# Three mixer gates computed as seven half-sized products by tokens

## The chip, the cores and the metric

The kernel runs on one core of one Trainium2 chip. The metric is device time in microseconds: 1072.74 us before, the median of 3 runs (1071.83 to 1073.14). Times inside the kernel come from one profiled execution.

## The reference

One decoder layer on 512 tokens of width 1024, in fp32. What matters here is the mixer's middle:

```python
proj = x @ w_in            # q/k/v columns of three branches, then 3 x 1024 gate columns
...
g = jax.nn.sigmoid(gates).reshape(B, S, N_BRANCHES, D)
merged = (g[:, :, 0] * (o_da @ w_branch_da) + g[:, :, 1] * (o_sb @ w_branch_sb)
          + g[:, :, 2] * (o_dl @ w_branch_dil))
return merged @ w_out
```

`o_da`, `o_sb` and `o_dl` (512 x 512 each) are the outputs of differential, stick-breaking and dilated attention. A layer norm of alpha * x + mixer(x) follows, then a squared-ReLU MLP (4096 wide), an embedding term with a gate of its own (sigmoid(x W_g), 1024 x 1024), and a second layer norm.

## The kernel before

**Arithmetic.** Each fp32 operand is split in a high half (cast to fp32r) and a low half (what the cast lost), and a product is three matmuls into one PSUM bank: high x high, high x low, low x high. For weights `split_next` does this: a cast on ScalarE (line 235) and a subtraction on VectorE (line 238) turn a raw tile of 128 x 1024 into `wh` and `wl`. Such a tile of 512 KB is called a chunk.

**Items.** The program is a list of items, made first and then walked in one loop (lines 1472 to 1525). An item is a run of matmuls into one bank (`mm`) and an evacuation (`ev`), which is issued when the next item begins. The items are, in order: 59 projections of q, k and v (main_order), of 24 matmuls each; the mixer gates (24 items `gate` of 24 matmuls each, columns in partitions, tokens along the free axis) with the branch products (24 items of 12 matmuls, `branch_items`) between them, two blocks of 128 columns ahead; the output projection (`wout_items`, 8 items of 24); the embedding's gate and the embedding (`wg_items`, `ple_items`); the MLP. Walking the list, `step` advances the attention heads, which are generators; a yield inside `mm` is one more step.

**Loads.** `fill` issues loads of raw tiles on SyncE's queue (SP) as far as raw tiles are free: 4 of them (RAW). `pump` splits up to 7 chunks (RING) ahead of the last freed one. A load waits in SP's queue until a split has freed its tile, and what is issued behind it on SP waits too.

**Seven products.** The embedding's gate and the MLP already use a scheme by which a product of 2 x 2 blocks takes seven half-sized products instead of eight. It needs sums of weight blocks. `totals` lists them, and `add` issues one at a time while the items go by: a copy of a block to a DRAM tile on SP's queue, then sums into it by an accumulating DMA on GpSimd's queue (POOL, line 176). `add` is called once per 3 units of item size from item 24 on. The sums of the activation blocks are made in SBUF, in `ln1_gen`, from transposes of the normed tokens.

**Merging.** For each of 8 column blocks the evacuation of a branch product applies the sigmoid to the gate (`gate_sig`, tied behind the last exponential of the differential attention), multiplies and adds; after the third branch the block is split in halves (`mh`, `ml`), and these stand still in the output projection without a transpose.

**Places.** 48 SBUF tiles of 128 x 512 are shared under the tag "s"; two large tiles (tags XH and XL) hold the halves of x transposed, and later those of the normed tokens; two PSUM banks `mm` and six `at`.

Of the kernel before, what the change touches and what calls it, by code (L numbers as in the profile page):

```python
# [17 lines left out]
P = 128  # L18
# [16 lines left out]
def main_order():  # L35
# [14 lines left out]
    for j in range(8):  # L50
        for i in range(3):
            o += [("T", "gate", 8 * i + j)]
# [3 lines left out]
def trunk(tc, a, out):  # L56
    nc = tc.nc
    es = ExitStack()
    with es:
# [7 lines left out]
        NSLOT = 48  # L67
# [74 lines left out]
        RING, RAW = 7, 4  # L142
        ORDERED, AHEAD = 17, 4
        loads, sums, chunks, placed = [], deque(), [], []
# [7 lines left out]
        def totals(quads):  # L152
# [5 lines left out]
            for o, i, more in ((0, 0, False), (2, 1, False), (0, 1, True), (2, 3, True), (1, 3, False), (3, 2, False)):  # L158
                for (q, x) in zip(quads, t):
                    sums.append((x[o], q[i], more))  # L160
            for o in (1, 3):
                for x in t:
                    sums.append((x[o], x[0 if o == 1 else 1][:, :], True))
            return [{1: q[0], 2: q[2], 3: q[3], 4: x[3], 5: x[0], 6: x[1], 7: x[2]} for q, x in zip(quads, t)]
# [3 lines left out]
        def add():  # L168
            if not sums:
                return  # L170
            t, s, more = sums.popleft()
            if not more:
                wide = [x.rearrange("(a b) m -> a (b m)", b=4) for x in (t[:, :], s)]
                nc.sync.dma_start(*wide)
                return
            i = nc.gpsimd.dma_start(t, s, accum_op=OP.add, max_dma_last_dim=2048)  # L176
            tc.add_manual_dep(getattr(i, "ins", i), casts[0].name, mybir.DependencyInfo(
                mybir.DependencyClass.Sync, mybir.DependencyReason.DATA), reason="one sum at a time")

        def chunk_of(s):  # L180
            c = {"from": s, "w": s["w"]}
            s["uses"] += 1
            chunks.append(c)
            return c
# [4 lines left out]
        def fill():  # L189
            while st["dma"] < len(loads):  # L190
                s = loads[st["dma"]]
                while any(t is s["src"] for t, _, _ in sums):
                    add()
# [75 lines left out]
        gate_raw = {}  # L269
# [16 lines left out]
        def t_evac(name, j):  # L286
            def ev(ps):
# [5 lines left out]
                elif name == "gate":  # L293
                    t = slot("graw")
                    cp(t, ps)
                    gate_raw[j] = t
# [75 lines left out]
        for kind, name, j in order[2:]:  # L372
            if kind == "T":
                if name == "gate":
                    continue
# [10 lines left out]
        sg = {}  # L386

        last_exp = [None]

        def gate_sig(i, j):  # L390
            t = gate_raw.pop(8 * i + j)

            with tc.issue_after(last_exp[0]):
                nc.scalar.activation(t, t, AF.Sigmoid)
            sg[i, j] = t

        def branch_items(j, between=()):
            c1 = chunk(a["wb1"][j].rearrange("p k m -> p (k m)"), 1024)
            c2 = chunk(a["wb2"][j].rearrange("p k m -> p (k m)"), 512)
            for n, i in enumerate((1, 2, 0)):  # L400
                if n == 2:
                    for t in between:
                        t_item(*t)
                    if j == 0:
                        first_da.append(len(items))
                def mm(ps, i=i):
                    c = c2 if i == 2 else c1
                    for k in range(4):
                        s = slice(((i % 2) * 4 + k) * P, ((i % 2) * 4 + k) * P + P)
                        h, lo = oTs[4 * i + k]  # L410
                        mm3(ps, c["h"][:, s], c["l"][:, s], h, lo, k == 0, k == 3)

                def ev(ps, i=i, n=n):
                    gate_sig(i, j)
                    g = sg.pop((i, j))
                    nc.vector.tensor_mul(g, g, ps)
                    if n == 0:
                        merged[j] = g
                    else:
                        nc.vector.tensor_add(merged[j], merged[j], g)  # L420
                    if n == 2:
                        m = merged[j]
                        h = slot("mh", F32R)
                        lo = slot("ml", F32R)
                        nc.scalar.copy(h, m)
                        nc.vector.tensor_sub(lo, m, h.bitcast(F32))
                        merged[j] = (h, lo)
                item([c1, c2] if n == 2 else [], mm, ev, need=[c1, c2], size=2)

        first_branch = [None]  # L430
        first_da = []
        LEAD = 2
        gates = [(j, i) for j in range(8) for i in range(3)]
        for j in range(LEAD):
            for i in range(3):
                t_item(nt, "gate", 8 * i + j)
                nt += 1
        first_branch[0] = len(items)
        for j in range(8):

            gs = [(nt + i, "gate", 8 * i + j + LEAD) for i in range(3)] if j + LEAD < 8 else []
            nt += len(gs)
            branch_items(j, gs if j == 0 else ())
            if j:
                for t in gs:
# [1178 lines left out]
```

## Time and profile before

| What | Value |
|---|---|
| median of 3 runs | 1072.74 us (1071.83 to 1073.14) |
| the profiled execution, its own time and its span | 1073.58 us, 1071.8 us |
| TensorE busy, instructions | 1056.0 us (99%), 5543 |
| VectorE, ScalarE busy | 719.9 us (67%), 528.3 us (49%) |
| moved by DMA | 203.87 MB, 190 GB/s on average |

In the lines of the page, a row of a group gives line, engine and operation, out<-in by tile names, shapes, and the count after x; then busy time and mean length of one in ns, then the idle time of the engine ahead of them and what ended it. A row of busy time by stretch gives start:end, length, then each engine's busy time with its instructions, the granted TensorE clock, the DMA engines' busy share and GB/s. A row of single instructions gives start and length in us. Bars of matmuls overlap, so their length is not what one costs. The projections end near 445 us, gates and branches run to 646 us, the output projection to 691, the embedding with its gate to 744.

### The profile page before, as it was taken

The page shows a single profiled execution, that of the slowest core. Times are in us where ns is not written, and L with a number is a line of the kernel's source. Part 1 is how long each engine was busy: PE and PEld are TensorE (multiplying, and loading weights), DVE is VectorE, ACT ScalarE, POOL GpSimd, SP SyncE. Part 2 cuts the span into 40 slices and gives each one's busy share as a digit, 9 for nine tenths or more (in the row PEclk, how much of TensorE's full clock was granted, in tenths as well). Part 3 has the DMA queues.
Part 4 walks back from the last instruction along what each step waited for, and adds up shares of the span by engine and source line. Part 5 has one row for each costly group of instructions (what it writes and reads, how often), then busy time and mean ns, then how long its engine had stood idle before and what let it go on. Part 6 is the DMA issues. An engine that isn't in the chain of part 4 may idle for free. (4 is left out here: it accounts for less than half of the span.)

```text
span 1071.8 us, 14697 instructions
## 1 busy us (share of the span) xinstructions
PE 1056.0 (99%) x5543; PEld 907.8 (85%) x5543; DVE 719.9 (67%) x1264; ACT 528.3 (49%) x866; POOL 83.0 (8%) x106
## 2 busy tenths in 40 slices
PE   8999999999999999999999999999999999999996
PEld 6888788999888888888888888888989989989985
DVE  5988577656443756655444445898786787787786
ACT  5665445435232545545333333375666567557551
POOL 0000200010011101011101110100100010000000
PEclk9999999999999999999999999999999999999999
DMA  7643545393777647575798757349989895655722
GB/s 275 189 175 123 174 166 134 122 255 98 236 217 199 192 139 209 172 204 163 202 259 226 189 160 243 110 132 279 245 215 258 253 257 194 196 177 178 236 79 79
DMA packets 61624, 203.87 MB, mean 190 GB/s; under 512 B 7387, under 2 KB 8299, under 8 KB 60465
## 3 DMA queue, kind: packets, MB, share of 16 engines
q1 hardware_dynamic: 41536, 164.03, 43.9%
q0 software_dynamic: 19440, 37.98, 20.5%
q8 instruction: 43, 0.70, 0.3%
q10 hardware_dynamic: 576, 0.92, 0.2%
q14 instruction: 29, 0.23, 0.1%
HBM read 200.78 MB, written 73.42 MB: 256 GB/s over the span
## 5 line engine op out<-in xcount | busy, mean ns | idle before, releaser
L235 ACT CAST wh<-raw 128x1024 fp32r<-128x1024 f32 (+1 forms) x231 | 238.9, 1036 | 296.6 <-PE mm L88 159.5
L238 DVE TENSOR_TENSOR wl<-raw,wh 128x1024 fp32r<-128x1024 f32 (+1 forms) x231 | 277.2, 1205 | 141.0 <-ACT wh L235 137.1
L87 PE MATMUL mm<-xhT,wh 128*128 128x512 f32 x496 | 196.4, 396 | 0.0
L89 PE MATMUL mm<-xhT,wl 128*128 128x512 f32 x496 | 194.2, 392 | 0.0
L88 PE MATMUL mm<-xlT,wh 128*128 128x512 f32 x496 | 194.0, 391 | 0.0
L89 PEld LDWEIGHTS mm<-xhT,wl 128*128 128x128 f32 x496 | 93.2, 188 | 19.6
L87 PEld LDWEIGHTS mm<-xhT,wh 128*128 128x128 f32 x496 | 93.3, 188 | 19.3 <-issue 1.1
L88 PEld LDWEIGHTS mm<-xlT,wh 128*128 128x128 f32 x496 | 93.3, 188 | 17.9
L744 PE MATMUL mm<-x1hT,wh 128*128 128x256 f32 x256 | 72.5, 283 | 2.4 <-DVE cut L756 2.4
L746 PE MATMUL mm<-x1hT,wl 128*128 128x256 f32 x256 | 72.5, 283 | 0.0
L745 PE MATMUL mm<-x1lT,wh 128*128 128x256 f32 x256 | 72.5, 283 | 0.0
L348 PE MATMUL mm<-wh,xhT 128*128 128x512 f32 x160 | 64.8, 405 | 0.0
L350 PE MATMUL mm<-wh,xlT 128*128 128x512 f32 x160 | 63.2, 395 | 0.0
L349 PE MATMUL mm<-wl,xhT 128*128 128x512 f32 x160 | 63.0, 394 | 0.0
L744 PE MATMUL mm<-xs,wh 128*128 128x256 f32 x192 | 54.5, 284 | 0.0
L745 PE MATMUL mm<-xs,wh 128*128 128x256 f32 x192 | 54.4, 283 | 0.0
L746 PE MATMUL mm<-xs,wl 128*128 128x256 f32 x192 | 54.3, 283 | 0.0
L176 POOL DMA_DIRECT2D total<-total x34 | 30.2, 954 | 278.7 <-ACT wh L235 233.1
L744 PEld LDWEIGHTS mm<-x1hT,wh 128*128 128x128 f32 x256 | 49.1, 192 | 2.8 <-issue 2.6
L745 PEld LDWEIGHTS mm<-x1lT,wh 128*128 128x128 f32 x256 | 49.1, 192 | 0.3
L746 PEld LDWEIGHTS mm<-x1hT,wl 128*128 128x128 f32 x256 | 49.2, 192 | 0.0
L350 PEld LDWEIGHTS mm<-wh,xlT 128*128 128x128 f32 x160 | 37.9, 237 | 3.9
(388 smaller groups left out, 2187.1 us busy)
## 6 DMA issues: line engine op xcount, KB each, us to landing
raw<-total SPq DMA_DIRECT2D x68, 512.0 KB, 4.3
raw<-in_wt_dram SPq DMA_DIRECT2D x62, 512.0 KB, 4.8
total<-total POOLq DMA_DIRECT2D x34, 512.0 KB, 9.5
total<-in_wu_dram SPq DMA_DIRECT2D x32, 512.0 KB, 6.8
total<-in_wd_dram SPq DMA_DIRECT2D x28, 512.0 KB, 6.6
raw<-in_wd_dram SPq DMA_DIRECT2D x25, 512.0 KB, 4.5
raw<-in_wu_dram SPq DMA_DIRECT2D x24, 512.0 KB, 4.6
raw<-in_wv_dram SPq DMA_DIRECT2D x20, 512.0 KB, 4.5
```

Source lines behind the costliest of these rows:

```text
L87: nc.tensor.matmul(ps, wh, xh, start=start, stop=False, skip_group_check=True)
L88: nc.tensor.matmul(ps, wh, xl, start=False, stop=False, skip_group_check=True)
L89: nc.tensor.matmul(ps, wl, xh, start=False, stop=stop, skip_group_check=True)
L176: i = nc.gpsimd.dma_start(t, s, accum_op=OP.add, max_dma_last_dim=2048)
L235: i = nc.vector.tensor_copy(h, raw) if c.get("dve") else nc.scalar.copy(h, raw)
L238: i = nc.vector.tensor_sub(lo, raw, h.bitcast(F32))
L348: nc.tensor.matmul(ps, x1, c["h"][:, s], start=k == 0, stop=False)
L349: nc.tensor.matmul(ps, x1, c["l"][:, s], start=False, stop=False)
L350: nc.tensor.matmul(ps, x2, c["h"][:, s], start=False, stop=k == 7)
L744: nc.tensor.matmul(o, c["h"][:, s], h, start=first, stop=False, skip_group_check=True)
L745: nc.tensor.matmul(o, c["h"][:, s], lo, start=False, stop=False, skip_group_check=True)
L746: nc.tensor.matmul(o, c["l"][:, s], h, start=False, stop=last, skip_group_check=True)
```

## The change

- The three gates become 14 items each of 12 matmuls (`seven`): tokens stand still, weights move, and seven products (numbered 1 to 7) with two groups of 128 tokens each give the four blocks of a gate. A bank is held over products 1, 6, 7, 4 in an `at` bank (`chain`).
- x's block sums are made by `x_load` (quarters of x loaded again, 8 loads of 256 KB) and `x_sum` (sum, cast, lower half), hooked to the items at and after the first gate. Gate tiles stay in "s" until used.
- The first gate (stick-breaking) has its four weight sums made by DMA. For the other two (`mixed`) only two sums are made by DMA; products 6 and 4 add a raw tile to the one of product 5 in SBUF (`plus`, a tensor_add in `split_next`), with weights ordered 1, 5, 6, 3, 4, 7, 2 and used in the order 1, 5, 6, 3, 7, 4, 2.
- Order: gate, gate, dilated branch, gate, then the branches of differential and stick-breaking attention. The dilated branch runs ahead of the point where all attention has ended.
- Branch products are by tokens too: 8 items of 12 matmuls each. Attention outputs are kept whole and split shortly before use (`halves`). The sigmoid has no tie to the exponentials any more.
- Merged tokens are transposed (`turn`, 32 transposes) into tiles under the tags XH and XL, which the output projection reads; `fold4` puts the normed tokens' halves in the same place afterwards. The output projection has a yield in its middle.
- `add` keeps two lists: copies (on SP, each issued after the last load) up to 24 ahead of the sums, and alone before item 23; it starts at item 7, with rates by stretch (one per 2.3, 5, 3.2, 2.4 or 5.5 units of item size).
- 5 raw tiles instead of 4, 46 tiles "s" instead of 48. The one-hot rows are loaded on SP with the constants, at item 4, instead of on POOL's queue.

```diff
-        NSLOT = 48
+        NSLOT = 46
...
-        RING, RAW = 7, 4
+        RING, RAW = 7, 5
...
+            if mixed:
+                t = [(new(), new()) for _ in quads]
+                for o in range(2):
+                    for q, x in zip(quads, t):
+                        copies.append((x[o], q[3 * o]))
+                for o in range(2):
+                    for q, x in zip(quads, t):
+                        sums.append((x[o], q[1]))
+                return [{1: q[0], 2: q[2], 3: q[3], 5: x[0], 7: x[1]} for q, x in zip(quads, t)]
...
+        def add(only=False):
+            if copies and (only or moved[0] < moved[1] + LEAD):
+                moved[0] += 1
+                t, s = copies.popleft()
                 wide = [x.rearrange("(a b) m -> a (b m)", b=4) for x in (t[:, :], s)]
-                nc.sync.dma_start(*wide)
...
+                with tc.issue_after(st["load"]):
+                    nc.sync.dma_start(*wide)
+            elif sums and not only:
+                moved[1] += 1
+                t, s = sums.popleft()
+                i = nc.gpsimd.dma_start(t, s, accum_op=OP.add, max_dma_last_dim=2048)
...
+            if c["plus"]:
+                raw = c["from"]["raw"]
+                nc.vector.tensor_add(raw, raw, c["plus"]["raw"])
+                c["plus"]["uses"] -= 1
...
+        def seven(ws, ops, fin, two):
...
+                def mm(ps):
+                    q = slice(r * P, r * P + P)
+                    for k in range(4):
+                        c = cs[k // 2]
+                        s = slice((k % 2) * 512, (k % 2) * 512 + 512)
+                        h, lo = operand(ops, p, k, q)
+                        nc.tensor.matmul(ps, h, c["h"][:, s], start=k == 0 and begins, stop=False,
+                                         skip_group_check=True)
+                        nc.tensor.matmul(ps, h, c["l"][:, s], start=False, stop=False, skip_group_check=True)
+                        nc.tensor.matmul(ps, lo, c["h"][:, s], start=False, stop=k == 3 and ends,
+                                         skip_group_check=True)
...
+            def weights(p):
+                if 6 in ws:
+                    return [chunk(w, 1024) for w in ws[p]]
+                base, more = {6: (5, 3), 4: (5, 2)}.get(p, (p, None))
+                for q in (base, more):
+                    if q and q not in raw:
+                        raw[q] = [load(w, 1024) for w in ws[q]]
+                return [chunk_of(raw[base][c], more and raw[more][c]) for c in range(2)]
...
+                if 6 not in ws:
+                    made = {p: weights(p) for p in (1, 5, 6, 3, 4, 7, 2)}
+                    for p in (1, 5, 6, 3, 7, 4, 2):
+                        for r in range(2):
+                            one_item(p, r, made[p], {4: made[4] + made[7], 7: []}.get(p))
+                    return
...
+            nc.vector.tensor_tensor(src, i, j, op=o)
+            nc.scalar.copy(h, src)
+            nc.vector.tensor_sub(lo, src, h.bitcast(F32))
+
+        GATES = (1, 2, 0)
+        gate_w = [block_weights("wga", i, n > 0) for n, i in enumerate(GATES)]
...
+        gate(0)
+        gate(1)
+        branch(2, False)
+        gate(2)
+        first_branch = len(items)
+        branch(0, False)
+        branch(1, True)
...
+        def turn(tt):
+
+            yield
+            if not mT:
+                mT.extend(one.tile([P, 8, 512], F32R, name=nm(n), tag=n, bufs=1) for n in ("XH", "XL"))
+            q = slice(tt * P, tt * P + P)
+            for half in range(2):
+                tp = at_bank()
+                for b in range(4):
+                    nc.tensor.transpose(tp[:, b * P:b * P + P], merged[tt, half][:, b * P:b * P + P], ident)
+                t3 = tp.rearrange("p (k t) -> p k t", k=4)
+                h, lo = [b[:, 4 * half:4 * half + 4, q] for b in mT]
+                nc.scalar.copy(h, t3)
+                nc.vector.tensor_sub(lo, t3, h.bitcast(F32))
+            yield
...
-            if n >= 24 and not wout_at + 2 <= n < wout_at + 16:
+            if n >= 7 and not wout_at + 5 <= n < wout_at + 20:
                 due[0] += it["size"]
-                while due[0] >= 3:
-                    due[0] -= 3
-                    add()
+                rate = 2.3 if n < gates_at else 5 if n < gates_at + 14 else 3.2 if n < first_branch else 2.4 if n < wout_at else 5.5
+                while due[0] >= rate:
+                    due[0] -= rate
+                    add(n < 23)
```

More of the change, by code (lines that the diff above doesn't have):

```diff
@@ L385, in trunk @@
         merged = {}
[L386 to L407, printed above, removed]
+        at = {}
@@ L428, in branch_items @@
[L428 to L445, printed above, removed]
-                    t_item(*t)
+                        nc.tensor.matmul(ps, h[:, q], c["h"][:, s], start=k == 0, stop=False)
```

399 lines of the change are left out of this document (222 added, 177 removed).

## The prediction

> **What bounds the kernel now.** I read the head of the page first, then busy time by stretch, then single starts on TensorE.
>
> ```profile
> PE 1056.0 (99%) x5543; PEld 907.8 (85%) x5543; DVE 719.9 (67%) x1264; ACT 528.3 (49%) x866; POOL 83.0 (8%) x106
> ```
> ```profile
> core 0: us, PE busy (x) PEld busy (x) DVE busy (x) ACT busy (x) POOL busy (x), PEclk, DMA share, GB/s
> ...
> 25.00:445.00 420.00, 419.47 (x2068) 355.33 (x2067) 277.10 (x640) 201.56 (x390) 33.56 (x42) 1.00 0.59 175
> 445.00:510.00 65.00, 65.00 (x325) 54.37 (x324) 35.46 (x79) 32.45 (x71) 9.11 (x10) 1.00 0.66 182
> 510.00:646.00 136.00, 136.00 (x602) 112.70 (x601) 62.59 (x76) 43.65 (x57) 14.45 (x17) 1.00 0.78 206
> ...
> 691.00:744.00 53.00, 52.17 (x240) 42.56 (x239) 49.04 (x73) 33.07 (x53) 4.54 (x5) 1.00 0.70 204
> 744.00:1072.00 328.00, 316.98 (x2040) 290.17 (x2039) 252.15 (x327) 191.09 (x262) 16.71 (x20) 0.99 0.68 198
> ```
>
> TensorE is busy in every stretch until the tail, at a granted clock of 1.00. The mixer gates and the branch products run from 445 to 646 us, and there it never pauses; VectorE and ScalarE have room. So a matmul that is removed there is time, and whatever is added matters only if it makes TensorE wait. A busy TensorE alone does not give the price of a matmul, since the bars overlap. Starts do:
>
> ```profile
> 646.10 0.39 PE L519 MATMUL mm<-wh,mh 128*128 128x512 f32 x1
> ...
> 683.95 0.39 PE L521 MATMUL mm<-wh,ml 128*128 128x512 f32 x1
> 684.18 1.03 PE L567 MATMUL at<-ident,xn 128*128 128x128 f32 x8
> 684.97 0.47 PE L519 MATMUL mm<-wh,mh 128*128 128x512 f32 x1
> 685.29 0.39 PE L520 MATMUL mm<-wl,mh 128*128 128x512 f32 x1
> ```
> ```profile
> L519 PE MATMUL mm<-wh,mh 128*128 128x512 f32 x56 | 21.8, 389 | 0.0
> L521 PE MATMUL mm<-wh,ml 128*128 128x512 f32 x56 | 21.8, 389 | 0.0
> L520 PE MATMUL mm<-wl,mh 128*128 128x512 f32 x56 | 21.8, 389 | 0.0
> ```
>
> Between 646.10 and 684.18 us there are 3 x 56 = 168 starts: 38.08 / 168 = **0.2267 us** for a 512-wide matmul, though its bar is 0.39 long. Eight transposes take 0.79 us, and the matmul behind them hands over after 0.32 instead of 0.23: **0.88 us** for eight.
>
> **The change, part by part.** *Gate matmuls.* Before, 24 items of 24 matmuls: 576. After, three gates of 7 products x 2 row groups x 4 k x 3 terms = 168 each: 504, all 512 wide. Removed: 72 x 0.2267 = **16.3 us**. The branch products stay 288 matmuls of 512 and the output projection 192; which operand stands still changes, the width doesn't.
>
> *Transposes.* The merged branches now come out with tokens in rows and must be turned for the output projection: 4 x 2 x 4 = 32 transposes, 4 x 0.88 = **+3.5 us**, all on TensorE. Net so far -12.8.
>
> The Trainium skill (TensorE: Matmul & The Clock Gate, section "Wait — 56ns, not 53.3ns?") gives a warm matmul N / 2.4 GHz plus about 2.5 ns, 215.7 ns at 512 and 55.6 ns at 128. By that the two terms would be -15.5 and +1.8, an estimate of -13.7; this trace has 227 and some 110 ns, and the rows decide.
>
> *Weights and their halves.* Splits (line 235 on ScalarE, 238 on VectorE) go from 24 + 8 + 8 half-sized ones to 42 + 12, and in the two mixed gates products 6 and 4 add a second raw tile first: 8 adds of 128x1024. The operand sums of x are 8 sums and 8 lower halves on VectorE at 512 wide, 8 casts on ScalarE.
>
> ```profile
> L238 DVE TENSOR_TENSOR wl<-raw,wh 128x1024 fp32r<-128x1024 f32 (+1 forms) x231 | 277.2, 1205 | 141.0 <-ACT wh L235 137.1
> L235 ACT CAST wh<-raw 128x1024 fp32r<-128x1024 f32 (+1 forms) x231 | 238.9, 1036 | 296.6 <-PE mm L88 159.5
> ```
> ```profile
> L238 DVE TENSOR_TENSOR wl<-raw,wh 128x1024 fp32r<-128x1024 f32 (+1 forms) x11 | 11.9, 1078 | 9.1 <-ACT wh L235 6.3 <-PE at L1278 2.8
> ...
> L98 DVE COPY graw<-mm 128x512 f32<-128x512 f32 x4 | 2.8, 692 | 4.6 <-PE mm L89 4.6
> ...
> L416 DVE TENSOR_TENSOR graw<-graw,mm 128x512 f32<-128x512 f32 x3 | 2.1, 688 | 3.2 <-PE mm L89 2.9 <-ACT graw L394 0.3
> ```
>
> An add reads and writes as much as the lower half: 1.2 us. An item of 12 matmuls is 12 x 0.2267 = 2.72 us and uses one chunk. The hardest place is the first gate and the first 8 items of the second, where the differential attention is still running: counting its yields against the items, its last block ends at item 81, 22 items after the gates begin. Its share of VectorE is what the stretch 445 to 510 holds beside splits and gates, 35.5 - 11.9 - 2.8 - 2.1 = 18.7 us. With 22 splits (26.5), 4 adds (4.8), 12 evacuations and 16 operand steps at 0.69 (19.3) that makes 69 us of VectorE against 22 x 2.72 = 60 us of gate matmuls and the attention's own time on TensorE. That is what the stretch 445 to 510 holds beside its wide matmuls, three lines with as many starts as this one, 3 x 79 x 0.2267 = 53.7 of 65 us:
>
> ```profile
> 445.00:510.00 65.00, 30.54 (x79) 1.00 0.66 182
> ```
>
> So 11 us, and VectorE has 69 us of work in 71: 97%. Seven chunks are split ahead and cover a lag of 8 us. The nearest row is the same seven-product form at 691 to 744: VectorE 49.0 of 53 us, TensorE waits 0.83. I take that for each gate, **+2.5 us**. Lower bound: 0, as in 510 to 646. Upper bound: VectorE reaches only the share of that row, 0.925, in the hard place: 69 / 0.925 = 75 against 71, 4 more, so +6.5.
>
> *The turned tiles.* They take over the place of x, and the first layer norm's split takes it over from them; so that split can no longer begin while the output projection still reads. Before, it ran under the last item:
>
> ```profile
> 684.82 1.08 ACT L551 CAST x1hT<-at 128x512 fp32r<-128x512 f32 x2 [15.70 <-PE at L567]
> ```
> ```profile
> 707.46 0.39 PE L656 MATMUL at<-wh,xs 128*128 128x512 f32 x1
> 707.69 0.39 PE L611 MATMUL mm<-wh,pTh 128*128 128x512 f32 x1
> ```
>
> Cover gone, TensorE waits for the last bar to end (0.39 in place of 0.23) and one cast (half of 1.08, about 0.6), and for the lower half soon after two matmuls: **+1.0 us**. Lower bound 0, because products of another kind are slipped between (line 611 in the second fence); upper bound 2.4, with both casts and a lower half each of 0.69 in a row.
>
> *Queues.* 10 more loads, 16 more copies and 16 more sums of 512 KB; 8 loads of x quarters. The one-hot rows move from POOL's queue to SP's, where 3 more issues stand ahead of the early loads; copies begin at item 7 instead of 24, on SP, each behind the last load.
>
> ```profile
> DMA  7643545393777647575798757349989895655722
> ...
> q1 hardware_dynamic: 41536, 164.03, 43.9%
> q0 software_dynamic: 19440, 37.98, 20.5%
> ...
> raw<-total SPq DMA_DIRECT2D x68, 512.0 KB, 4.3
> ...
> total<-in_wu_dram SPq DMA_DIRECT2D x32, 512.0 KB, 6.8
> ```
>
> A load or copy takes 43.9% of 1071.8 us / (164.03 / 0.524) = 1.5 us of all 16 engines, a sum 20.5% / (37.98 / 0.524) = 3.0. Added: 26 x 1.5 + 16 x 3.0 = 87 us, which spread over the kernel lifts the share from 0.65 to 0.74. I cost it at 0: it lies under matmuls with 7 chunks split and 5 raw tiles ahead. Early, 43 more operations before item 59 (about 97 us) bring 25 to 445 from 0.59 to 0.82, below the eight to nine tenths that the first row holds in its slices 27 to 32, from 724 us on, where a chunk is due every 2.7 us and TensorE is full. The upper bound is the rival of the slower side below. Table switches: 24 sigmoids with a tie behind the last exponential become 24 behind the end of attention; nothing on TensorE waited for them, 0.
>
> **The sum**, against the profiled execution's own 1073.58 us: -16.3 + 3.5 + 2.5 + 1.0 = -9.3, so 1064.3; that execution lies 0.84 above the median of 1072.74, so **1063.4 us** for the median. With the unknown terms at their ends (0 and 0, 6.5 and 2.4): 1059.9 to 1068.8.
>
> **The rivals.** *Nothing new waits*: 1072.74 - 12.8 = 1059.9. For it, the 136 us without a pause at 510; against it, the pauses of the only stretch that has this form. If its two named waits went too, 0.7 and 2.4, 1056.8.
>
> ```profile
> PE mm L744 <- DVE cut L756: 2.4, 1, 2.4
> ...
> PE at L653 <- ACT cut L675: 0.7, 1, 0.7
> ```
>
> *VectorE becomes the bound* in the hard place and again where branches, turning and splits meet (per branch item two 0.69 steps and half a split, 2.0 of 2.72 us, before 8 more steps for the turning): the upper bounds, 1068.8.
>
> *Slower: raw tiles turn round too slowly in the two mixed gates.* Five raw tiles hold ten loads, and the tile of the first sum is held for three products. Product 4 may be split from 5.4 us after a gate's start, when product 1 frees its halves; then add, cast and lower half (1.2 + 1.04 + 1.2 = 3.4), the load into the freed tile, the same again for its second chunk, one more load, and cast and lower half 2.2 for product 7. With loads that land in 4.3: 5.4 + 2 x 7.7 + 2.2 = 23.0 against 8 x 2.72 = 21.8 when TensorE wants it, 1.2 late. If each load stands in SP's queue behind a copy and lands only with it (6.8 and 4.3): 5.4 + 2 x 14.5 + 2.2 = 36.6, 14.8 late; two gates 30, 1093. It decides from (9.3 + 2.1) / 2 = 5.7 us late a gate, that is from a landing of 6.6 us on. For it: SP's queue is in order and always stands at its head,
>
> ```profile
> SPq L207 <- DVE wl L238: 764.1, 205, 25.8
> ```
>
> and behind the waiting load stand copies and later loads, for which splits wait. Against it: the tile of product 3 comes free earlier and can take the load, and the second half of the kernel feeds a chunk in 2.7 us with four tiles.
>
> *The change does not do what it says* could only mean that products were not half-sized; 504 follows from its loops, so I give it nothing.
>
> **How the numbers follow.** The forecast, between 1060.5 and 1067: 0.57. Nothing waits, 1060.5 and below: 0.19. VectorE bound, 1067 to 1071: 0.12. Raw tiles, above 1071: 0.12. The likeliest is 1063.4. What a measurement can tell from no change is 0.2%, 2.1 us, so the border is 1070.6 and 1074.9. Faster is 0.57 + 0.19 + 0.10 = 0.86; the raw tiles' case puts 0.03 of itself inside the border, which with VectorE's other 0.02 makes 0.05 for the same; slower 0.09. The range goes from 1057.5 (near the end with the two old waits gone) to 1071, which leaves out 0.12 above and about 0.03 below.
>
> **What would show it.** 504 gate matmuls at 0.227, 32 new transposes at 0.11, so PE's instructions fall by 40. PE waits for VectorE's `cut` or `wl` of some 0.8 us in each gate; one wait of about 1 us before the first product of the embedding's gate, ended by the cast of `x1hT`. If raw tiles decide, PE waits in the two mixed gates for `wl` of product 7, and loads there land later than 6.6 us. If VectorE decides, it is above 0.95 busy with PE below. A saving that shows more than 13 us would prove that the old kernel lost time in a place that I read as full.

## The result and the profile after

The changed kernel takes **1083.89 us** (median of 4 runs, 1083.39 to 1084.44) against 1072.76 for the kernel before beside it: a ratio of 1.0105, interval 1.0088 to 1.0123. It is 11.1 us slower, where 9.3 us less were forecast. The profiled execution took 1084.44 us with a span of 1082.7, 10.9 more than before.

First the head of the page after: busy time by engine, then the granted TensorE clock and the DMA engines' share in 40 slices of 27 us.

```profile
PE 1050.2 (97%) x5503; PEld 899.5 (83%) x5503; DVE 761.6 (70%) x1316; ACT 559.8 (52%) x908; POOL 96.1 (9%) x119
...
PEclk9999999999999999699999999999999999999999
DMA  7455664628879596745985997348889899896712
```

TensorE has the 40 instructions less that were forecast and is busy 5.8 us less, but the span is longer. One slice of the clock is at 6, the 17th, from 433 us on. Busy time by stretch (start:end, length, each engine's busy time with its instructions, granted clock, DMA share, GB/s) shows the same place:

```profile
25.00:425.00 400.00, 398.08 (x1955) 336.38 (x1955) 248.53 (x576) 184.04 (x352) 38.32 (x47) 1.00 0.66 194
425.00:475.00 50.00, 34.51 (x146) 27.91 (x145) 30.84 (x69) 24.01 (x52) 3.21 (x4) 0.80 0.62 191
475.00:646.00 171.00, 170.91 (x791) 141.28 (x790) 126.67 (x190) 93.35 (x147) 19.82 (x21) 1.00 0.84 243
...
707.00:760.00 53.00, 51.47 (x243) 42.33 (x243) 48.51 (x72) 33.54 (x52) 2.81 (x3) 1.00 0.64 201
760.00:1083.00 323.00, 313.17 (x2010) 286.42 (x2008) 248.33 (x323) 187.62 (x257) 25.49 (x30) 0.99 0.74 218
```

From 425 to 475 us, where the last projections meet the first gate, TensorE is busy 34.5 of 50 us at a clock of 0.80. From 475 on, in both mixed gates and all branches, it does not pause. TensorE's waits name what ended the pauses, and a finer cut of the stretch shows the clock:

```profile
PE at L1379 <- DVE lg L1374: 9.2, 2, 8.8
PE mm L451 <- DVE da_qb L105: 3.5, 1, 3.5
PE at L135 <- ACT da_ka L126: 2.5, 1, 2.5
PE at L451 <- ACT cut L460: 1.4, 1, 1.4
```
```profile
425.00:435.00 10.00, 6.80 (x29) 5.30 (x28) 6.39 (x11) 4.77 (x10) 1.23 (x2) 0.90 1.13 308
435.00:440.00 5.00, 4.63 (x18) 3.42 (x16) 0.00 (x0) 0.00 (x0) 0.00 (x0) 0.86 0.92 235
440.00:445.00 5.00, 0.00 (x0) 0.00 (x0) 0.77 (x2) 0.40 (x1) 0.00 (x0) 0.82 1.06 393
445.00:450.00 5.00, 1.56 (x8) 1.59 (x9) 3.74 (x8) 1.63 (x5) 0.00 (x0) 0.50 0.95 332
450.00:455.00 5.00, 2.52 (x7) 1.51 (x6) 1.99 (x3) 2.13 (x3) 0.00 (x0) 0.50 0.00 0
455.00:460.00 5.00, 4.00 (x11) 3.45 (x12) 4.60 (x20) 2.82 (x8) 0.00 (x0) 0.50 0.31 108
```

The books: 50 - 34.5 = 15.5 us of pause; 1.56 + 2.52 + 4.00 = 8.1 us of work at half clock cost 4.0; the two rows at 0.90 and 0.86 cost 6.80 x 0.10 + 4.63 x 0.14 = 1.3. That is 20.8. With 1.1 for the hand-over of the turned tiles and 0.7 more at the embedding's gate (1.4 against 0.7) it makes 22.6; the span's 10.9 and the 12.8 that the forecast takes off for matmuls and transposes make 23.7. So 1.1 us are not accounted for.

What VectorE did in the pause stands in its single instructions; behind the brackets is the idle time and what ended it:

```profile
434.11 0.08 DVE L1363 DVE_READ_ACCUMULATOR2_ANT mx<- 128x1 f32 x1
443.79 0.69 DVE L542 TENSOR_TENSOR xq<-xq,xq 128x512 f32<-128x512 f32 x1 [9.60 <-DMA xq<-in_xT_dram]
444.40 0.16 DVE L1367 TENSOR_SCALAR mx<-mx 128x2 f32<-128x2 f32 x1
```

The order of each engine's list of instructions is fixed when the program is built. Line 542 is the first operand sum of x. It stood in VectorE's list ahead of the steps of an attention block (1367 to 1374) that TensorE's transposes waited for, and its operands were still in flight. Line 1367 needs only what line 1363 had left at 434.19, and yet it runs at 444.40, behind line 542. ScalarE's and SP's instructions in the 20 us before, and the row of the DMA issues for the quarters (KB each, median us to landing):

```profile
422.16 2.94 ACT L255 CAST wh<-raw 128x1024 fp32r<-128x1024 f32 x3
428.32 1.04 ACT L255 CAST wh<-raw 128x1024 fp32r<-128x1024 f32 x1 [3.23 <-PE mm L85]
429.27 0.58 ACT L122 ACTIVATE da_ka<-mm 64x512 fp32r<-64x512 f32 x1
```
```profile
404.88 19.92 SPq L223 DMA_DIRECT2D raw<-total  x4
...
427.44 4.06 SPq L527 DMA_DIRECT2D xq<-in_xT_dram  x4
```
```profile
xq<-in_xT_dram SPq DMA_DIRECT2D x8, 256.0 KB, 13.3
```

SP took 19.9 us over four loads of raw tiles: the row runs from the issue of the first to that of the last, and each waited until VectorE's lower half had freed a tile, 8.8 us at the longest. In that time the DMA engines ran dry; these are their busy tenths from 375 to 432 us in 40 slices, nearly idle from 416 to 421 and from 422 to 425:

```profile
DMA  0048991029999999999699863799300091089994
```

Then two loads, two copies and the quarters of x went out together, and a quarter took 13.3 us to land at a DMA share of 0.9 to 1.1. Three casts of weights ran at 422, a fourth waited 3.2 us for its place in the ring, and the evacuation of da_ka, whose matmuls had ended near 421, stood behind it until 429.3. That makes three suspects: late quarters (or full DMA engines), the place of the sum on VectorE, the places of the casts on ScalarE.

### The profile page after: what moved, and what is told of

Read it like the earlier page. It is cut to its first block, busy times and chain, and to the rows that moved or that the text cites. A ratio compares the mean times of both kernels' runs of the same rounds, so it can differ in the third digit from the quotient of the medians.

```text
span 1082.7 us, 14807 instructions
## 1 busy us (share of the span) xinstructions
PE 1050.2 (97%) x5503; PEld 899.5 (83%) x5503; DVE 761.6 (70%) x1316; ACT 559.8 (52%) x908; POOL 96.1 (9%) x119
## 4 chain that ended last, share of the span: by engine, by line
PE 84%; DVE 6%; DMA 4%; ACT 2%; issue 2%; POOL 0%; SPq 0%; DVEq 0%; POOLq 0%; ACTq 0%
PE mm L84 5%; PE mm L85 5%; PE mm L86 5%; PE mm L869 5%; PE mm L871 5%; PE mm L870 5%; PE mm L363 3%; PE mm L364 3%; PE mm L365 3%; PE at L453 2%; PE at L451 2%; PE at L454 2%; PE mm L957 2%; PE mm L956 2%; PE mm L958 2%
## 5 line engine op out<-in xcount | busy, mean ns | idle before, releaser
L258 DVE TENSOR_TENSOR wl<-raw,wh 128x1024 fp32r<-128x1024 f32 x245 | 296.5, 1221 | 126.6 <-ACT wh L255 123.4
L255 ACT CAST wh<-raw 128x1024 fp32r<-128x1024 f32 x245 | 255.3, 1050 | 229.3 <-PE mm L870 42.8
L84 PE MATMUL mm<-xhT,wh 128*128 128x512 f32 x304 | 121.5, 400 | 0.9 <-DVE da_klb L105 0.7
L86 PE MATMUL mm<-xhT,wl 128*128 128x512 f32 x304 | 120.1, 395 | 0.2 <-DVE wl L258 0.2
L85 PE MATMUL mm<-xlT,wh 128*128 128x512 f32 x304 | 120.0, 395 | 0.0
L869 PE MATMUL mm<-XH,wh 128*128 128x256 f32 x256 | 72.5, 283 | 1.2 <-DVE cut L881 1.2
L871 PE MATMUL mm<-XH,wl 128*128 128x256 f32 x256 | 72.4, 283 | 0.0
L870 PE MATMUL mm<-XL,wh 128*128 128x256 f32 x256 | 72.4, 283 | 0.0
L869 PEld LDWEIGHTS mm<-XH,wh 128*128 128x128 f32 x256 | 49.1, 192 | 1.6 <-issue 1.4
L870 PEld LDWEIGHTS mm<-XL,wh 128*128 128x128 f32 x256 | 49.1, 192 | 0.3
```

The source lines that it names most:

```text
L84: nc.tensor.matmul(ps, wh, xh, start=start, stop=False, skip_group_check=True)
L85: nc.tensor.matmul(ps, wh, xl, start=False, stop=False, skip_group_check=True)
L86: nc.tensor.matmul(ps, wl, xh, start=False, stop=stop, skip_group_check=True)
L255: i = nc.vector.tensor_copy(h, raw) if c.get("dve") else nc.scalar.copy(h, raw)
L258: i = nc.vector.tensor_sub(lo, raw, h.bitcast(F32))
L869: nc.tensor.matmul(o, c["h"][:, s], h, start=first, stop=False, skip_group_check=True)
```

## The experiments

All compare with the kernel before in the same batch of runs (1070.6 to 1072.2 us); "the changed kernel" is 1083.89. Since the kernel before differs by 1.6 us between batches, differences of less than 2 us between runs of different batches are not read.

**Earlier loads, no loads, no copies and sums near the gates.** Three single edits, and the first and third together.

```diff
 e1, e4
-            hook(gates_at - 2 + kp, lambda kp=kp: x_load(kp))
+            hook(gates_at - 8 + kp, lambda kp=kp: x_load(kp))
 e2 (no x_load)
-            a11, a21, a12, a22 = [xq[kp, i] for i in (1, 5, 2, 4)]
+            a11, a21, a12, a22 = [xhT[:, k:k + 2, t].bitcast(F32) for k, t in ...]
 e3, e4: no add() for gates_at - 10 <= n < gates_at + 4
```

> The changed kernel with the 8 loads of x quarters hooked 6 items earlier. Theory A (the quarters come late: VectorE's queue stands 9.6 us before the first operand sum, attention's steps stand behind it, TensorE pauses 15.9 us in all between 425 and 460 us and its clock falls to half): the wait of 8.8 us before the transposes of lg is gone, the clock stays at 1.0, about 1065 us (1083.9 less some 14 of the 15.9 us and some 5 us of half clock). Theory B (too little room: VectorE and the 46 tiles are too full where gates and attention overlap, and the quarters are only what is seen to wait): another instruction waits in the same place, 1078 us or more.

> The changed kernel without the quarters' loads: the operand sums take the high halves of x that lie in SBUF already (and in product 7 one other block), with as many instructions on VectorE and ScalarE as before; the low halves of x are left out of the sums, so the output is not the reference's. Theory A: no wait for loads can be left, 1063 to 1066 us, clock 1.0. Theory B: the work on VectorE is the same, 1078 us or more.

> The changed kernel with no copies and sums issued from 10 items before the gates to 4 items into them; they follow later. If the quarters are late because the DMA engines are full (landing 13.3 us), they land in about 6 and the pause falls by about 7 us, with part of the half clock: 1072 to 1076 us. If they are late because they stand in SP's queue behind loads that wait for a raw tile, little changes: 1081 us or more. Theory B: 1081 us or more.

> Both: quarters 6 items earlier and no copies and sums around the first gate. Theory A: as the run with the early quarters alone within 2 us, about 1065 us, since an early load does not mind 13 us. Theory B: 1078 us or more.

Measured: e1 **1081.16** (ratio 1.0087, 1.0067 to 1.0106), e2 **1082.64** (1.0099, 1.0081 to 1.0117), e3 **1092.49** (1.0187, 1.0172 to 1.0202), e4 **1095.99** (1.0223, 1.0208 to 1.0238). In e1 the wait had moved with the loads, and grown; first VectorE's instruction, then busy time by stretch:

```profile
407.58 0.69 DVE L542 TENSOR_TENSOR xq<-xq,xq 128x512 f32<-128x512 f32 x1 [17.17 <-DMA xq<-in_xT_dram]
```
```profile
395.00:405.00 10.00, 0.00 (x0) 0.00 (x0) 0.00 (x0) 0.00 (x0) 0.00 (x0) 0.64 1.05 272
```

The list of VectorE's instructions has the sum just behind the loads wherever these are, so loading earlier alone helps little: for 10 us no engine computed anything. In e2 the wait for x is gone, and TensorE waits for weights in its place (6.8 us in two waits for `wh`, ahead of product 7 of both mixed gates). In e3 and e4 the sums that had been put off were late for the MLP (13.9 and 13.3 us in three waits of its products).

The total of e3 hides what it did at the place itself. Its quarters land in 6.5 us, VectorE does not stand for x, the pause of 8.8 us is gone, and the second gate begins at 493.9 us, in the changed kernel at 508.4:

```profile
425.00:475.00 50.00, 46.81 (x226) 38.78 (x225) 42.11 (x100) 37.60 (x77) 2.27 (x2) 0.97 0.55 173
```

So the copies and sums that share the DMA engines with the quarters made them late, as the expectation of e3 had it. All four times lie in theory B's ranges, but its reason is not the one: in e3 VectorE has the same work to do there, and no other wait takes the place of the pause. But these transfers have little slack to give, and where the loads are moved (e1) or left out (e2) another wait does take it.

**The place of the sum, and room.** e5 is e1 with a tie that keeps the sum behind the last split issued one item ahead of the gates; e6 has the tie alone; e7 is e5 with all block sums of gates made in DRAM; e9 leaves the gates' copies and sums out.

```diff
 e5, e6, e7
-            nc.vector.tensor_tensor(src, i, j, op=o)
+            with tc.issue_after(mark[0]):
+                nc.vector.tensor_tensor(src, i, j, op=o)
+        hook(gates_at - 1, lambda: mark.__setitem__(0, st["low"]))
 e7
-        gate_w = [block_weights("wga", i, n > 0) for n, i in enumerate(GATES)]
+        gate_w = [block_weights("wga", i, False) for n, i in enumerate(GATES)]
 e9: totals() of the gates returns plain blocks; their places in copies and sums stay empty
```

> The quarters of x are asked for 8 items ahead of the gates instead of 2, and each operand sum on VectorE (line 542) may only be placed behind the last weight split that is issued one item ahead of the gates. Theory O (order: the first operand sum stands in VectorE's queue right behind its loads, wherever these are, and everything behind it waits for them): the pause of 16.5 us that the early loads alone showed goes, with the half clock behind it, so 1081.2 - 16.5 - 4 = about 1061 to 1066. Theory R (room: the 16 DMA engines are full round the first gate, and whatever needs a transfer there is late): the sum no longer waits for x, but weights come late in its place, as in the kernel without the loads; 1076 or more, with waits for the cast or the lower half of weights between 425 and 600 us of 15 us or more.

> The quarters of x are asked for 2 items ahead of the gates as in the changed kernel; only the operand sums are held behind the last weight split issued one item ahead of the gates. Theory O: the sums move one or two weight splits later, some 3 to 5 us, of the 9.6 us that VectorE stood; the rest of the pause stays, so 1075 to 1080. Theory R: no change, 1082 to 1085, since the loads land in 13 us whatever stands behind them.

> As the early loads with held sums, and in all three gates every block sum is made in DRAM by a copy and an accumulating transfer, none in SBUF by VectorE: 8 adds of 1.2 us less on VectorE, 8 copies and 8 accumulating transfers more. Theory M (the mixed gates turn their raw tiles round too slowly): waits of the second and third gate go and it is 3 us or more faster than the early loads with held sums. Theory R: 8 x 1.5 + 8 x 3.0 = 36 us more of all 16 DMA engines, so 5 us or more slower than that kernel, with the waits at weights. Theory O: the same as that kernel within 2 us.

> The gates' 16 copies and 16 accumulating transfers are left out, and their places in the sequence stay empty; the products read the plain blocks in place of the sums, so the three gates hold wrong values: the sums of weight blocks are left out, the loads, the splits, VectorE's adds, the quarters of x and every matmul stay. Theory R: with 16 x 1.5 + 16 x 3.0 = 72 us less of all 16 DMA engines ahead of and in the gates, their mean share from 380 to 460 us falls from about 1.0 to 0.8 or less, the quarters land in 6 us or less, and the pause of 8.8 us with the half clock behind it goes: 1062 to 1068. Theory O: VectorE still stands at the first operand sum for 5 us or more, 1076 to 1081.

Measured: e5 **1063.04** (0.9916, 0.9901 to 0.9932), e6 **1084.97** (1.0120, 1.0103 to 1.0136), e7 **1074.89** (1.0026, 1.0014 to 1.0037), e9 **1073.37** (1.0012, 1.0000 to 1.0024). Busy time in the stretch of the first gate in e5:

```profile
425.00:475.00 50.00, 49.77 (x254) 41.57 (x253) 46.52 (x116) 39.09 (x86) 3.17 (x3) 1.00 0.70 219
```

With the loads early and the sum late, both pauses are gone, and the kernel beats both others: 18.1 us below e1 by the tie alone. The transfers hardly got faster (a quarter lands in 11.4 us), so the loss can go with every byte left in place. The tie without the early loads does nothing: VectorE still stands at the first sum, for 9.8 us and behind the same instruction. In e9 there is room (DMA share 0.61 in place of 1.0 from 425 to 450 us), the quarters land in 6.5 us and the wait for x is gone, as in e3, but two other waits stay (TensorE's waits in e9),

```profile
PE mm L455 <- DVE da_qb L105: 3.7, 1, 3.7
PE at L135 <- ACT da_ka L126: 2.5, 1, 2.5
```

so theory R explains some 10 of the 24 us and theory O, as I had put it (the sum only), the same part; both missed e9's time. Theory M falls: more work for the DMA engines and less for VectorE made e7 11.9 us slower than e5. That is theory R's sign and size, but the longest wait, 4.3 us, is in the MLP and not for weights.

**The tie without loads, and later sums.** e10 is e2 with the tie; e11 moves the sums two items later and leaves the loads where the change has them.

```diff
 e11
+        hook(gates_at, lambda: x_ops.update(quarters(xhT, xlT)))
+        hook(gates_at + 1, lambda: mark.__setitem__(0, st["low"]))
-                hook(gates_at + 2 * n + kp, lambda kp=kp, p=p: x_sum(p, kp))
+                hook(gates_at + 2 + 2 * n + kp, lambda kp=kp, p=p: x_sum(p, kp))
```

> As the kernel without the loads of x quarters (operand sums from the high halves that lie in SBUF, product 7 with another block, so the lower halves' part of the sums is left out and product 7's values are wrong), and the sums on VectorE may only be placed behind the last weight split issued one item ahead of the gates. Without the tie that kernel took 1082.6, with VectorE making no weight split between 437 and 454.8 us because the sums and their casts stood ahead of it. Theory O (the order on VectorE and ScalarE decides, not the transfers): splits stand in their places again, 1060 to 1066. Theory W (weights come late in the mixed gates because five raw tiles turn round too slowly once nothing else holds the gates up): waits of 4 us and 3 us ahead of product 7 stay, 1072 to 1083.

> The quarters of x are asked for where the change asks for them, 2 items ahead of the gates; the operand sums are placed two items later each and the first of them only behind the last weight split issued one item into the gates, so it stands some 8 us later in VectorE's order, two items ahead of the product that reads it. Theory O: the quarters land in 13 us as before, but VectorE no longer stands for them; the pause of 8.8 us and the half clock behind it go, 1064 to 1070. Theory L (the loads themselves are what hurts, since eight more issues of 1 KB rows stand in SP's queue ahead of the weights of the first gate): weights come late, 1076 or more.

Measured: e10 **1083.34** (1.0106, 1.0089 to 1.0123), e11 **1078.73** (1.0064, 1.0049 to 1.0079). Both theories on the sum are too small. In e10 no transfer of x exists, and SP's queue still stands from 404.5 us on:

```profile
404.50 24.54 SPq L223 DMA_DIRECT2D raw<-total  x4
```

The DMA engines' busy tenths from 375 to 432 us in e10, in 40 slices, say that there was room; toward the end of the stand they are idle:

```profile
DMA  0039990059999999999999881999200280000079
```

ScalarE's list tells the difference. The casts of weights from 380 to 400 us, first in e5, then in the changed kernel:

```profile
381.99 2.93 ACT L255 CAST wh<-raw 128x1024 fp32r<-128x1024 f32 x3
```
```profile
384.07 1.05 ACT L255 CAST wh<-raw 128x1024 fp32r<-128x1024 f32 x1
392.74 2.00 ACT L255 CAST wh<-raw 128x1024 fp32r<-128x1024 f32 x2
```

In e5 three stand in a row ahead of an evacuation of da_ka (at 384.83). In the changed kernel one stands behind that evacuation (at 381.70) and two more behind the exponentials that follow. My reading, theory C below, was: casts that stand late keep raw tiles; loads wait for raw tiles on SP; what is behind them goes out in a burst. And in e11 the waits for da_ka and da_qb are as before, behind a cast that waits for its place.

**One chunk less ahead.** If the cast is too far ahead, splitting less far ahead should free ScalarE.

```diff
-            while n < most and st["split"] < len(chunks) and st["split"] < limit + RING:
+            while n < most and st["split"] < len(chunks) and st["split"] < limit + RING - st["less"]:
```

> The kernel with late sums (loads where the change has them, operand sums two items later), and from 8 items ahead of the gates to 4 items into them the weights are split one chunk less ahead (6 chunks in place of 7). In the kernel with late sums ScalarE stood 3.2 and 5.6 us at the cast of a weight chunk whose place TensorE had not yet freed, with the attention's casts of da_ka and da_qa behind it, and TensorE waited 2.5, 0.7 and 3.7 us for these. Theory S (ScalarE's order: a cast put too far ahead holds up the attention's casts): those waits go, 1078.7 - 7 = 1069 to 1073. Theory W (splits are what is short, as in the kernel without loads, where they were two or three chunks fewer at the first gate matmul): one chunk less ahead makes TensorE wait for weights instead, 1078 or more.

> The changed kernel, with the one chunk less ahead in the same stretch as its only edit. Theory S: the waits of 2.5 us for da_ka and 3.5 us for da_qb go, while VectorE still stands at the first operand sum for about 9 us: 1083.9 - 7 = 1075 to 1079. Theory W: 1084 or more.

Measured: e12 **1082.48** (1.0109, 1.0093 to 1.0124), e13 **1080.27** (1.0085, 1.0068 to 1.0101). The waits for da_ka (2.5) and da_qb (3.5) are still there in both, and so are ScalarE's at the casts (3.23 and 5.50 us): the edit asks for the casts an item later, but their place in ScalarE's list stayed ahead of the evacuations. So it did not take away what it was meant to, and says nothing on the theory. (What it did shorten in e13, the pause ahead of the transposes of lg from 8.8 to 4.5 us, was not forecast.)

**The casts ahead of the exponentials.** The edit that acts on the list itself: near the gates each exponential may only stand behind the last cast issued before it, in the changed kernel (e15), without loads of x (e16), with late sums (e17).

```diff
-                nc.scalar.activation(lg[m], lg[m], AF.Exp, ...)
+                with tc.issue_after(st["cast"]) if st["near"] else ExitStack():
+                    nc.scalar.activation(lg[m], lg[m], AF.Exp, ...)
```

> The changed kernel; from 12 items ahead of the gates to 2 items into them each exponential of the differential attention on ScalarE may only stand behind the last weight cast issued before it. Theory C (casts that stand too late in ScalarE's order keep raw tiles, so SP's queue stands some 20 us from 405 us on and the quarters of x then come in a burst and land in 13 us): SP's longest stand between 395 and 430 us falls below 10 us, the quarters land in less than 10 us, and of the 24 us that the stretch 425 to 475 lost at least half comes back: 1064 to 1073. Theory L (the loads of x in SP's queue are what hurts): 1080 or more.

> The kernel without the loads of x quarters (sums from the high halves in SBUF, product 7 with another block, so product 7's values are wrong and the lower halves' part of the sums is left out), with the same order for the exponentials. Theory C: SP's stand of 24.5 us from 405 us on goes, 77 splits are done at the first gate matmul in place of 74, and the waits for weights in the first gate go; 1060 to 1068. Theory W (five raw tiles are too few in the mixed gates): the waits ahead of product 7 in both mixed gates stay, 1073 or more.

> The kernel with late sums, with the same order for the exponentials. Theory C: the waits of 2.5, 0.7 and 3.7 us just ahead of the first gate go, and with them nearly all that is left: 1061 to 1068. Theory L: 1076 to 1080, as without it.

Measured: e15 **1079.78** (1.0076, 1.0061 to 1.0091), e16 **1071.10** (0.9991, 0.9982 to 1.0000), e17 **1077.97** (1.0057, 1.0041 to 1.0074). Without loads of x, where nothing else is in the way, the place of the casts is worth 11.5 us (e2 to e16, 1082.64 to 1071.10). But SP does not stand less. The row of four loads that reads 24.54 us in e10 reads 14.38 in e16, but it begins only when the first of them goes out, and the wait ahead of that one is 16.2 us in e16 and 5.7 in e10. SP's waits from 395 to 430 us (us in total, times, longest), first in e10, then in e16:

```profile
SPq L223 <- DVE wl L258: 26.2, 4, 8.8
SPq L223 <- DVE rr L1376: 9.4, 1, 9.4
```
```profile
SPq L223 <- DVE wl L258: 25.6, 3, 16.2
SPq L223 <- DVE rr L1375: 8.3, 1, 8.3
SPq L223 <- DVE mx L1370: 1.5, 1, 1.5
```

That is 35 us in both. What the edit brings is that the last of the four loads goes out 10 us earlier, at 418.7 in place of 428.7. In e15 none of theory C's three signs came: SP's longest wait grew to 16.2 us, the quarters land in 10.5, and 4.1 us come back. With the loads, the wait for x halves (VectorE in e15),

```profile
438.58 0.69 DVE L542 TENSOR_TENSOR xq<-xq,xq 128x512 f32<-128x512 f32 x1 [4.97 <-DMA xq<-in_xT_dram]
```

and the pair of waits for da_ka and da_qb stays, in e17 too, whose time is the one that theory L gave. So the place of the casts counts, but not by a shorter stand of SP as theory C had it, and it is not all.

**The casts behind the evacuations.** Near the gates each cast may only stand behind the last evacuation of an attention projection issued before it: in the changed kernel (e18), with late sums (e19), with late sums and the exponentials behind the casts (e20).

```diff
-                i = nc.vector.tensor_copy(h, raw) if c.get("dve") else nc.scalar.copy(h, raw)
+                with tc.issue_after(st["ev"]) if st.get("late") else ExitStack():
+                    i = nc.vector.tensor_copy(h, raw) if c.get("dve") else nc.scalar.copy(h, raw)
```

> The changed kernel; from 8 items ahead of the gates to 4 items into them each weight cast on ScalarE may only stand behind the last evacuation of an attention projection issued before it. Theory E (a cast that must wait for its place to come free stands ahead of the evacuation that TensorE needs): the waits of 2.5 us for da_ka and 3.5 us for da_qb go, with the half clock behind them; VectorE still stands at the first operand sum, so 1083.9 - 7 = 1074 to 1079. Theory L (the loads in SP's queue): unchanged, 1082 or more.

> The kernel with late sums, with the same place for the casts. Theory E: of 1078.7 the waits of 2.5, 0.7 and 3.7 us go with 1 to 2 us of half clock, so 1068 to 1072; what is left above 1063 is a wait of some 2 us of VectorE for the second half of x and 3 us in the mixed gates. Theory L: 1076 or more.

> Late sums, exponentials behind the casts, casts behind the evacuations, all together, with the loads of x where the change has them. Theory E and theory C together: the order of the kernel with early loads and held sums is had without moving the loads, 1062 to 1068. If the loads' place is what matters, 1074 or more.

Measured: e18 **1082.02** (1.0100, 1.0078 to 1.0122), e19 **1074.28** (1.0022, 1.0011 to 1.0033), e20 **1068.54** (0.9974, 0.9964 to 0.9985). In all three the waits for da_ka and da_qb are gone, as theory E had it, but all three times lie above its ranges: e18's is the one that theory L gave, e20's is 0.5 us above, and well below the 1074 that was to blame the place of the loads. In e18 the gain is eaten: with ScalarE out of the way, VectorE comes to the first sum 3 us earlier and stands there longer, and TensorE pauses once, for 12.3 us,

```profile
443.18 0.69 DVE L545 TENSOR_TENSOR xq<-xq,xq 128x512 f32<-128x512 f32 x1 [12.28 <-DMA xq<-in_xT_dram]
```

which I had not reckoned with. In e20, whose loads of x are where the change puts them, the stretch from 425 to 450 us is

```profile
425.00:450.00 25.00, 24.85 (x124) 20.21 (x122) 21.20 (x54) 19.12 (x43) 1.81 (x2) 1.00 0.97 302
```

TensorE full, at full clock, with the DMA engines as busy as in the changed kernel. The three edits take no work and no byte away; they change the order of two engines' lists, and take off 15.4 us. Late sums alone take off 5.2 us, with the exponentials behind the casts 5.9, with the casts behind the evacuations 9.6; the two edits of the casts without late sums were not run together. What e20 lacks to e5 (5.5 us) are in part waits of 1.7 and 1.5 us in the first gate and 1.3 us ahead of product 7 of the third; why these come was not tried.

## Why the prediction was wrong, and where it was right

**Right: what the change takes off.** 40 instructions less on TensorE, as counted. The eight transposes of a row group start within 0.79 us here too:

```profile
638.63 1.03 PE L709 MATMUL at<-ident,cut 128*128 128x128 f32 x8
639.42 0.47 PE L592 MATMUL mm<-wh,oTh 128*128 128x512 f32 x1
```

In e5, where the order does no harm, the span is 1060.8 against 1071.8: 11.0 less. That is 12.8 less 1.1 for the hand-over and 0.7 for the embedding's gate. Two other waits changed and nearly cancel: 2.4 us at the MLP's first product became 1.2, and one of 1.0 us at 59 us is new.

**Right: the hand-over of the turned tiles.** +1.0 was forecast, one wait ahead of the embedding's gate. It is there, 1.09 us, behind the gate's first two matmuls, ended by the lower half of line 728 and not by the cast:

```profile
702.72 0.39 PE L453 MATMUL mm<-wl,XH 128*128 128x512 f32 x1
704.20 0.50 PE L454 MATMUL mm<-wh,XL 128*128 128x512 f32 x1 [1.09 <-DVE XL L728]
```

**Too high: +2.5 for waits in the gates.** In e5 no wait of the three gates is longer than 0.3 us; there is only that of the embedding's gate, grown from 0.7 to 1.4. VectorE as the bound did not come either: in e5, in the 71 us from the start of the first gate (436.6), it is busy 62.8 us, where the forecast had 69, with TensorE at 70.8.

**Wrong: "I cost it at 0", the step on queues.** It argued with averages: 87 us of transfers spread over the kernel, a share of 0.82 before the gates, 7 chunks split and 5 raw tiles ahead as cover. The mean from 25 to 445 us came out lower than that, 0.68; what counted were the 20 us from 425 on, at 1.06. The cover depends on a cast being run when its raw tile has landed, and the lists of ScalarE and VectorE decide that. In the changed kernel the casts stand late, SP takes 20 us over four raw loads, the DMA engines first idle and then get everything at once, and the quarters of x, which I had costed at nothing with the rest, land in 13.3 us while an instruction that needs them stands at the head of VectorE. The step should have asked, for each new load, which instruction waits for it, what is behind that one in its engine's list, and what it costs if the load takes twice its usual time. The price, 20.8 us, is also beyond the upper end of my range, since none of the rivals was at this place: the forecast of VectorE's work in the hard place added up busy time and left out standing.

**The slower rival, raw tiles in the two mixed gates,** did not decide: TensorE is busy 170.9 of 171 us from 475 on, and undoing the mixing (e7) costs 11.9. Its picture of SP's queue, a load that waits for a raw tile with others behind it, is what happened, but ahead of the first gate and to the quarters of x. Waits at the place that it names exist in other kernels, at a smaller size: ahead of product 7 of the third gate TensorE waits 2.8 us in e16, 2.4 in e18 and 1.3 in e20, and in e2 4.1 and 2.7 us in both mixed gates. Whether too few raw tiles bring these was not tried.

**Sigmoids without their tie** cost nothing, as forecast: no wait of TensorE is ended by one. But they do not all stand behind the end of attention: the first runs at 474.57, among the exponentials, and ScalarE switches tables five times between sigmoids and exponentials, 1.28 us each, where the kernel before did it three times.

**Open.** What set the order to be as it is in the changed kernel, and would have told it before, is not in a profile of the kernel before; that stays open here.

## What to carry over

When a change adds loads and steps that need them, price not their bytes but the place of the first instruction that waits: what stands behind it on its engine, and who waits for that. An edit that asks for a load earlier moves the wait along unless its consumer is held back too (1081.2 against 1063.0), and one that frees one engine can only bring it sooner to the next wait (e18). When the sum of removed work is certain and the time does not follow, look for the one stretch with a low clock and read three queues there side by side before blaming bandwidth alone: here fewer transfers at the place took off 10.5 us (e9), and another order with all of them, the loads of x earlier, took off 20.9 (e5).

## What the runs showed of the hardware

A pause costs more than its length. After the pause of 8.8 us TensorE ran from 448.4 to 460 us at half clock (with one more pause of 3.5 us in it), with 512-wide matmuls starting every 0.43 us in place of 0.227; a wait of 2.5 us ended at 431.04 did the same until 436:

```profile
435.75 0.63 PE L85 MATMUL mm<-xlT,wh 128*128 128x512 f32 x1
436.17 0.49 PE L86 MATMUL mm<-xhT,wl 128*128 128x512 f32 x1
436.50 0.39 PE L84 MATMUL mm<-xhT,wh 128*128 128x512 f32 x1
```

The Trainium skill (TensorE: Matmul & The Clock Gate, section "What's actually happening") has the clock fall to 4/8 after an idle window of about 3.4 us and rise after as long a busy one. The half clock agrees; here a pause of 2.5 us followed by one of 0.7 was enough, and the measurement decides.

A load of 256 KB took 6.5 us in the median to land in e9 (DMA share 0.6) and 13.3 us in the changed kernel (share about 1.0). A load of 512 KB in SP's queue waited 9.4 us for its raw tile in e10, until 428.7 us, and for most of that time the DMA engines had nothing to do: a full queue and an idle DMA engine are no contradiction.
